# One fused two-block network on one core: SSD decays moved off GpSimd, small matmuls issued as groups, and a planner that knows the array's tilings

## Chip, cores and metric

One core of a Trainium2 chip runs the whole program as one launch. The metric is the time on the device in microseconds. The kernel before was run three times: 3711.24, 3717.8 and 3721.67 us, median 3717.8 us.

## The reference

A token stream of 512 tokens and a context of 256 tokens, 1024 channels in fp32, go through a block of two layers and then through a second block. Layer 0 is a gated-delta mixer with a mixture of experts, layer 1 an SSD mixer with a mixture of experts; both are modulated by adaLN chunks (a vector times a weight of 1024 by 6144). The second block has an S5 mixer, a short convolution and a sparse attention side by side, and a gated feed-forward. Cut to what the change touches:

```python
# gated delta: the solve that the kernel does by blocks of 32, 64 and 128
lower = where(strict, einsum('nbhid,nbhjd->nbhij', kb, kc) * decay, 0.0)
sol = triangular_solve(eye + lower, rhs, lower=True, unit_diagonal=True)
# SSD, for each of 8 groups of 4 heads, forward and backward
acs = cumsum(dt_i * A, axis=1)
seg = where(tril, acs[:, :, None] - acs[:, None, :], -inf)
wts = einsum('btgn,bsgn->btsg', c_i, b_i)[..., None] * exp(seg) * dt_i[:, None]
y = einsum('btsgr,bsgrp->btgrp', wts, x_i) + ...
# adaLN
m = silu(cvec) @ w + b
```

## The kernel before

Channels lie on the partitions, tokens on the free axis. Large products are done with each fp32 operand split into a high and a low half (`mm3`: three matmuls); the halves of a weight are made on ACT (`wh`) and on DVE, for some SSD weights on POOL (`wl`). Small products are plain fp32 matmuls, which show as two records each in the trace. A stationary operand of 32 or 64 rows or columns takes a part of the 128 x 128 array; outputs on other partitions of PSUM go to other column parts, inputs on other partitions of SBUF to other row parts.

**The planner.** The program is recorded by the class `Rec`: each call on an engine becomes an operation with its predecessors and an estimated cost. `flush` orders what was recorded and only then issues it; there are some ten flushes, one for each stage. `schedule` is a list scheduler: at each step it takes, for each engine, the first operation by rank among those that can start earliest, within a tolerance `tol`; the rank is the program's position less `beta` times the length of the chain that hangs on the operation. `flush(trials)` makes an order for each pair (beta, tol) and issues the one whose planned end is first. TensorE is planned as one engine that does one matmul after another; a matmul of few columns has a cut cost. Each engine runs its instructions in the order issued; buffers come from rings (`bufs`), PSUM has eight tiles. All DMAs are issued on SP.

**Gated-delta stage** (`gdn`, 110 to 790 us). For each of eight heads: projections, norms (`ssq`: four matmuls with ones in 32 columns), the products that make L, then the inverse of 48 blocks of 32 x 32 on POOL, and two steps that join blocks of 32 and of 64. A step has a product `pB`, a copy on ACT and a product `pU`, and for 64 also transposes `pT`; each takes six tiles of time and four (or two) diagonal blocks, which lie in different row and column parts of the array. The loop is over blocks outside and time tiles inside. A scan of six steps in two directions follows. Four of six adaLN rounds are put between heads as `side` work: a round is, for each of eight k, a weight load of 1 MB and four matmuls of 32 columns, c = 0 to 3, each recorded for itself.

**SSD stage** (`ssd`, groups from 1506 to 2100 us). For each of eight groups: for each of four heads, two rows of cumulated decays are broadcast from DRAM (R), POOL subtracts `cs` from each, DVE takes the minimum (W), ACT the exponential; POOL makes Dm = mask x dt for one direction, DVE adds the other in four steps of 128 columns and multiplies W by Dm. Then projections, states, `cb` = B'C (copied to SBUF by ACT), W times cb on DVE, and the products `py` of 64 columns, two heads side by side.

The experts' stages (842 to 1506 and up to 2755 us), the second block's mixers and its feed-forward are changed in their order alone.

Of the kernel before, what the change touches and what calls it, by code (L numbers as in the profile page):

```python
# [52 lines left out]
class Rec:  # L53
# [4 lines left out]
    def __init__(self, nc, tc):  # L58
        self.nc, self.tc = nc, tc
        self.tiles, self.ops = {}, []  # L60
        self.access = {}
        for e in ("tensor", "vector", "scalar", "gpsimd", "sync"):
            setattr(self, e, Proxy(self, e))
        self.free_at = {e: 0.0 for e in ("tensor", "vector", "scalar", "gpsimd", "sync")}
        self.dma_free = 0.0
        self.slot_times = {}
        self.seen = set()
        self.npool = 0
        self.stacks, self.left = {"left": [], "right": []}, {"left": [], "right": []}
# [55 lines left out]

    def add(self, engine, method, a, k):
        reads, writes = [], []
# [8 lines left out]
        i = len(self.ops)  # L136
# [16 lines left out]
        if engine == "tensor":  # L153
            r = ww[0]
            key = r[0] + "#pe"
            q = (key, r[1] // 32 * 32, -(-r[2] // 32) * 32, 0, 1)
            lst = self.access.setdefault(key, [])
            preds.update(j for j, _, z in lst if q[1] < z[2] and z[1] < q[2])
# [3 lines left out]
        self.ops.append(dict(e=engine, m=method, a=a, k=k, preds=preds, names=names, cost=self.cost(engine, method, reads, writes, a, k), psum=any(self.tiles.get(r[0], (0, 0, 0))[2] for r in rr + ww)))  # L162
# [54 lines left out]
    def flush(self, trials=((0.0, 30.0),)):  # L217
# [54 lines left out]
        self.span, self.seq, self.free_at, self.dma_free, times = best  # L272
        self.slot_times.update(times)
        self.seen.update(uses)
        for i in self.seq:
            o = ops[i]
            getattr(getattr(self.nc, o["e"]), o["m"])(*o["a"], **o["k"])  # L277
        self.done, self.ops, self.access = ops, [], {}

    def schedule(self, static, beta, tol):  # L280
# [13 lines left out]
        for t, lst in order.items():  # L294
            for nm in lst:
                if nm in self.seen:
                    got.add(nm)
                    slots[t].remove(max(slots[t]))
                    alloc[t].add(pos[nm])
                    nxt[t] = pos[nm] + 1  # L300
        npred = [len(o["preds"]) for o in ops]
# [17 lines left out]
        while len(seq) < n:  # L319
            best = None  # L320
            for e, c in cand.items():
                fe = free_at[e]
                eb = None
                for r in c[: self.WINDOW]:
                    i = by[r]
                    st = max(fe, ready[i])
                    if eb is not None and st >= eb[0] - tol:
                        continue
                    for nm in ops[i]["tiles"]:
                        if nm in got:  # L330
# [12 lines left out]
            if best is None:  # L343
                return math.inf, seq, free_at, dma_free, slots
# [35 lines left out]
        return max(end), seq, free_at, dma_free, slots  # L380
# [169 lines left out]
def gdn(K, H, apply, w, ba_w, conv_w, a_log, dt_b, norm_g, scr, bscr, tscr, rscr, side, xc, w_out, gate, route):  # L550
# [111 lines left out]
    for h in range(NH):  # L662
# [27 lines left out]
        for j, a in enumerate((q, k_)):  # L690
            sq = per.tile([128, TT], F32, name="sq", tag="th", bufs=2)
            s.activation(sq, a, AF.Square, scale=0.5)
            for f in range(2):
                c = 32 * (2 * j + f)
                pe.matmul(pq[c:c + 32, :], K.ones[:, 0:32], sq[:, f * 384:(f + 1) * 384], start=True, stop=True)
# [94 lines left out]
        for m in (32, 64):  # L790
# [3 lines left out]
            else:  # L794
                p = K.ps([128, 6, m], "pT")
                for d, ra, ca in cut:
                    for t in range(6):
                        if d:
                            pe.matmul(p[ra, t, :], U[ra, d, t, ra], K.ident[ra, ra], start=True, stop=True, skip_group_check=True)
                        else:  # L800
                            pe.transpose(p[ra, t, :], U[ra, d, t, ra], K.ident[ra, ra])
# [4 lines left out]
            for d, ra, ca in cut:  # L806
                for t in range(6):
                    pe.matmul(p[ra, t, :], L[ca, t, ra], Ud[ca, 1 - d, t, :] if m == 32 else U[ca, d, t, ca], start=True, stop=True, skip_group_check=True)
# [3 lines left out]
            for d, ra, ca in cut:  # L812
                for t in range(6):
                    pe.matmul(p[ra, t, :], Tr[d][ra, t, :], B[ra, t, :], start=True, stop=True, skip_group_check=True)
# [102 lines left out]
    nc.flush(GDN_TRIALS)  # L917
# [4 lines left out]
GDN_TRIALS = ((0.4, 0.0),)  # L922
# [4 lines left out]
class Mod:  # L927
# [9 lines left out]
    def round(self, r):  # L937
# [4 lines left out]
        for k in range(KT):  # L942
            wt = K.wtile(self.w[r, k], [128, 4, 512])
            for c in range(4):
                nc.tensor.matmul(p[32 * c:32 * c + 32, :], self.sc[:, k, :], wt[:, c, :], start=(k == 0), stop=(k == KT - 1))
# [161 lines left out]
def moe(K, X, ws, regions, gate, routed, keep_next, gain, fill, side):  # L1107
# [159 lines left out]
    nc.flush(((0.0, 0.0),) if two else ((0.6, 30.0),))  # L1267
# [149 lines left out]
def ssd(K, H, apply, w, wz, w_dt, conv_w, conv_b, a_log, dt_b, d_skip, norm_g, w_out, gate, keep, scr, rscr, side, route):  # L1417
# [46 lines left out]
    K.softplus(dt, a, tmp, sh, "W", 4)  # L1464
# [8 lines left out]
    for dst, ms in ((cs, (mid[:, 0, :], mid[:, 1, :])), (ea, (K.m_le, K.m_ge)), (we, (K.m_gt, K.m_lt)), (et, (K.ones, K.ones))):  # L1473
# [5 lines left out]
        s.activation(dst, p, AF.Copy if dst is cs else AF.Exp)  # L1479
    for j, x in enumerate((cs, ea)):  # L1480
# [4 lines left out]
        s.activation(rows, p.rearrange("p t i -> p (t i)"), AF.Copy)  # L1485
# [5 lines left out]
    for g in range(8):  # L1491
# [3 lines left out]
        for r in range(4):  # L1495
            h = 4 * g + r
            R = []
            for d in range(2):
                x = tmp.tile([128, 4, 128], F32, name="R", bufs=4)
                nc.sync.dma_start(x.rearrange("p t i -> p (t i)"), dbc(rscr[32 * d + h], 128))  # L1500
                g_.tensor_tensor(x, x, cs[:, :, 32 * d + h:32 * d + h + 1].to_broadcast([128, 4, 128]), op=OP.subtract)
                R.append(x)
            W = tmp.tile([128, 4, 128], F32, name="W", bufs=4)
            v.tensor_tensor(W, R[0], R[1], op=OP.min)
            s.activation(W, W, AF.Exp)
            Dm = tmp.tile([128, 4, 128], F32, name="Dm", bufs=1)
            g_.tensor_tensor(Dm, K.m_le[:, None, :].to_broadcast([128, 4, 128]), dt[:, 0:4, h:h + 1].to_broadcast([128, 4, 128]), op=OP.mult)
# [80 lines left out]
        cbs = grp.tile([128, 4, 128], F32, name="cbs", bufs=2)  # L1588
        s.activation(cbs, pcb, AF.Copy)
        for W in Ws:  # L1590
            v.tensor_tensor(W, W, cbs, op=OP.mult)
        py = [K.ps([128, 512], "py") for _ in range(2)]
        for i in range(2):
            for t in range(4):
                for r in range(2):
                    h = 2 * i + r
                    pe.matmul(py[i][64 * r:64 * r + 64, t * 128:(t + 1) * 128], xt[:, t, h * 64:(h + 1) * 64], Ws[h][:, t, :], start=(t == 0), stop=(t == 3))
# [35 lines left out]
    nc.flush(((0.3, 30.0), (0.1, 0.0), (0.6, 0.0)))  # L1633
# [29 lines left out]
    nc.flush(((0.6, 30.0), (0.8, 30.0), (0.8, 120.0)))  # L1663
# [504 lines left out]
def mix_out(K, H, I, y5, yc, ya, keep, gain):  # L2168
# [44 lines left out]
    nc.flush(((0.6, 30.0),))  # L2213
# [7 lines left out]
def ffn(K, X, H, R, I, out):  # L2221
# [28 lines left out]
    nc.flush(((0.6, 30.0),))  # L2250
# [3 lines left out]
def block2(K, X, Rs, I, scr, par, e_par, uscr, keep, out):  # L2254
# [25 lines left out]
    nc.flush(((0.0, 30.0), (0.0, 60.0), (0.3, 60.0), (0.6, 60.0)))  # L2280
# [5 lines left out]
    nc.flush(((1.0, 30.0),))  # L2286
# [198 lines left out]
```

## Time and profile before

| | |
|---|---|
| median of three runs | 3717.8 us |
| the profiled execution's own time | 3719.51 us |
| span of its instructions | 3717.7 us |
| PE busy | 3442.1 us, 93%, 21457 instructions |
| DVE busy | 1914.3 us, 51% |
| ACT busy | 1105.9 us, 30% |
| POOL busy | 662.7 us, 18% |
| mean granted TensorE clock | 0.966 |
| DMA | 669.18 MB, mean 180 GB/s |

PE is TensorE's matmuls, PEld its weight loads, DVE VectorE, ACT ScalarE, POOL GpSimd, SP SyncE. A busy time is the union of an engine's instructions. All operations are recorded through one helper, so every row has the same line, L277, and instructions are told apart by their tiles, written out<-in. "128*32 128x512" means 128 rows and 32 columns of the array and a moving operand of 512 columns. A row with "x8" stands for eight instructions of one kind one after another.

### The profile page before, as it was taken

What the parts mean: (1) busy time and instruction counts of PE and PEld (TensorE: products, weight loads), DVE (VectorE), ACT (ScalarE), POOL (GpSimd) and SP (SyncE); (2) the same over time, 40 slices, a digit from 0 to 9 for tenths busy, and PEclk for the clock granted to TensorE, in tenths of its full rate; (3) what the DMA queues carried; (4) which work ended last, traced back from release to release, by engine and by line L of the source; (5) the groups of instructions that cost most, each with busy time, mean ns of one, the idle gap of its engine ahead of it and who ended that gap; (6) DMA issues with size and microseconds to landing.
All of it is one profiled execution on the core that took longest, in us unless ns stands there. A gap on an engine that the chain in (4) does not pass through costs nothing. (4 is left out here: it accounts for less than half of the span.)

```text
span 3717.7 us, 55087 instructions
## 1 busy us (share of the span) xinstructions
PE 3442.1 (93%) x21457; PEld 2310.9 (62%) x21457; DVE 1914.3 (51%) x4006; ACT 1105.9 (30%) x2270; POOL 662.7 (18%) x849
## 2 busy tenths in 40 slices
PE   7999998899999999889999779988879999999999
PEld 4777775656444454667777664332247657878887
DVE  4657754453223222798888551371254574445552
ACT  3355443423111111433333322020032343333331
POOL 0546544301000000154444011020001000000000
PEclk9989999899999999999999889999999999999999
DMA  5422137354888887343333349899972302333332
GB/s 193 151 54 66 54 85 244 123 187 162 348 313 322 333 321 298 115 119 102 115 106 101 129 181 365 357 369 410 420 214 77 120 1 91 94 105 85 97 87 87
DMA packets 251649, 669.18 MB, mean 180 GB/s; under 512 B 72156, under 2 KB 85612, under 8 KB 202236
## 3 DMA queue, kind: packets, MB, share of 16 engines
q1 hardware_dynamic: 251388, 665.66, 50.7%
q8 instruction: 169, 2.77, 0.3%
q14 instruction: 92, 0.75, 0.1%
HBM read 644.26 MB, written 21.30 MB: 179 GB/s over the span
## 5 line engine op out<-in xcount | busy, mean ns | idle before, releaser
L277 DVE TENSOR_TENSOR wl<-w,wh 128x512 fp32r<-128x512 f32 (+3 forms) x452 | 320.9, 713 | 443.2 <-PE fu L277 67.6
L277 ACT ACTIVATE wh<-w 128x512 fp32r<-128x512 f32 (+3 forms) x500 | 307.0, 621 | 620.8 <-PE fu L277 120.6
L277 PE MATMUL eg<-we,xs 128*32 128x512 f32 (+1 forms) x1536 | 374.2, 597 | 9.5 <-DMA we<-moe_w 8.3
L277 PE MATMUL eu<-we,xs 128*32 128x512 f32 (+1 forms) x1536 | 324.4, 595 | 7.6 <-DMA we<-moe_w 7.6
L277 PE MATMUL ey<-we,hTs 128*32 128x512 f32 (+1 forms) x1536 | 295.9, 599 | 12.0 <-ACT hTs L277 9.0
L277 PE MATMUL px<-H,wl 128*128 128x512 f32 (+1 forms) x768 | 271.3, 372 | 6.4 <-DVE wl L277 6.4
L277 PE MATMUL px<-H,wh 128*128 128x512 f32 (+1 forms) x768 | 272.9, 376 | 2.8 <-ACT wh L277 1.6
L277 PE MATMUL px<-H1l,wh 128*128 128x512 f32 (+1 forms) x768 | 272.8, 369 | 0.0
L277 PE MATMUL ec<-we,xs 128*32 128x512 f32 x1024 | 237.5, 594 | 0.0
L277 DVE TENSOR_TENSOR yl<-ey,yh 64x512 fp32r<-64x512 f32 x64 | 44.1, 689 | 330.7 <-ACT yh L277 330.1
L277 POOL TENSOR_TENSOR wl<-w,wh 128x512 fp32r<-128x512 f32 x48 | 64.4, 1345 | 738.0 <-DVE H1l L277 651.5
L277 PEld LDWEIGHTS eg<-we,xs 128*32 128x32 f32 (+1 forms) x1536 | 98.7, 119 | 139.8 <-issue 94.6
L277 DVE SCALAR_TENSOR_TENSOR eth<-eth,eg 128x512 f32<-128x512 f32 x32 | 22.0, 688 | 312.9 <-ACT eth L277 312.9
L277 PEld LDWEIGHTS eu<-we,xs 128*32 128x32 f32 (+1 forms) x1536 | 94.8, 119 | 139.7 <-issue 97.2
L277 PEld LDWEIGHTS ey<-we,hTs 128*32 128x32 f32 (+1 forms) x1536 | 98.6, 120 | 120.9 <-issue 60.9
L277 PEld LDWEIGHTS px<-H,wh 128*128 128x128 f32 x768 | 146.3, 194 | 30.3 <-issue 6.4
L277 PEld LDWEIGHTS px<-H,wl 128*128 128x128 f32 x768 | 145.2, 194 | 28.9 <-DVE wl L277 8.5
L277 PEld LDWEIGHTS px<-H1l,wh 128*128 128x128 f32 x768 | 145.2, 194 | 23.3 <-issue 4.6
L277 ACT ACTIVATE eth<-eg 128x512 f32<-128x512 f32 x32 | 19.1, 596 | 463.2 <-PE eg L277 434.4
L277 PE MATMUL eyc<-we,hcTs 128*32 128x256 f32 x1024 | 143.4, 379 | 0.0
L277 POOL TENSOR_TENSOR x<-D 48x30 f32<-48x30 f32 (+14 forms) x240 | 127.1, 530 | 90.8 <-DVE D L277 73.9
L277 POOL TENSOR_TENSOR D<-D,x 48x30 f32<-48x30 f32 (+14 forms) x240 | 133.6, 557 | 17.9
(1041 smaller groups left out, 7816.1 us busy)
## 6 DMA issues: line engine op xcount, KB each, us to landing
we<-moe_w SPq DMA_DIRECT2D x384, 1024.0 KB, 7.2
w<-ada_w SPq DMA_DIRECT2D x192, 256.0 KB, 4.9
w<-w_gu SPq DMA_DIRECT2D x88, 256.0 KB, 3.0
w<-gdn_w SPq DMA_DIRECT2D x64, 256.0 KB, 3.2
w<-ssd_w SPq DMA_DIRECT2D x64, 256.0 KB, 4.0
R<-ssd_rows SPq DMA_DIRECT2D x64, 256.0 KB, 4.7
w<-w_mix SPq DMA_DIRECT2D x48, 256.0 KB, 2.7
w<-w_dn SPq DMA_DIRECT2D x40, 256.0 KB, 2.6
```

What stands on the lines that cost most here:

```text
L277: getattr(getattr(self.nc, o["e"]), o["m"])(*o["a"], **o["k"])
```

## The change

1. *SSD.* The sums `cs` are stored negated. W is made from R[0] by ACT (Identity with `cs` as bias, four instructions of 128 columns) and R[1] is joined by DVE in one step each (add cs, minimum). POOL's two kinds of decay work go. The masks are multiplied into cb (two products of 512 columns a group, from PSUM), and Dm is made after cb: ACT scales one direction by dt, DVE adds the other, and one product W by Dm replaces two. W's ring has 6 tiles in place of 4; R's has 3 and serves Dm too.
2. *Groups.* Matmuls recorded inside `nc.together()` are one operation of the plan and are issued one after another: ssq, pT, pB, pU, adaLN's four and py. For pT, pB and pU the loop is over time tiles outside and blocks inside. The transposes of pT are all matmuls by the identity.
3. *Planner.* `array` gives for each matmul its tiling, its place in the array and a time; `schedule` lets places of one tiling run side by side and adds 94 ns where the tiling changes.
4. *Trials.* Every flush takes the same 15 pairs in place of lists of one to four.

```diff
+    @contextmanager
+    def together(self):
+        assert self.run is None
+        self.run = []
+        yield
+        self.run = None
...
+        if not self.run:
+            self.run.append(len(self.ops))
+            self.record(self.run[0], engine, method, a, k)
+            self.ops[-1]["more"] = []
+        else:
+            self.record(self.run[0], engine, method, a, k)
...
+    SWITCH = 94.0
+    @staticmethod
+    def array(method, a):
...
+        size = lambda x: 32 if x <= 32 else 64 if x <= 64 else 128
+        lhs, n = a[1], free(a[2])
+        rows, cols = size(lhs.ap[0][1]), size(free(lhs))
+        r0, c0 = (x.offset // x.ap[0][0] % 128 if x.ap[0][0] else 0 for x in (lhs, a[0]))
+        wide = lhs.dtype in (F32, F32R)
+        two = lhs.dtype == F32 and method != "transpose"
+        d = (2 if two else 1) * n / 2.4 + (13.5 if lhs.dtype == F32R else 4.0)
+        if wide and cols == 128:
+            d = max(d, 109.0 * free(lhs) / 128 if lhs.dtype == F32 else 94.0)
+        elif wide:
+            d = max(d, 58.0 if cols == 64 else 30.0)
+        else:
+            d = max(d, 28.0)
+        return (rows, cols), (r0 // rows, c0 // cols), (2 if two else 1) * d
...
-    def flush(self, trials=((0.0, 30.0),)):
+    TRIALS = tuple((b, t) for b in (0.0, 0.2, 0.4, 0.6, 1.0) for t in (0.0, 30.0, 90.0))
+    def flush(self, trials=TRIALS):
...
+                    if e == "tensor":
+                        tiling, place, _ = ops[i]["pe"][0]
+                        st = max(st, held.get(place, 0.0) if tiling == mode else drained + self.SWITCH)
...
+            elif e == "tensor":
+                fin = at = st
+                for tiling, place, t in o["pe"]:
+                    if tiling != mode:
+                        if mode is not None:
+                            at = max(at, drained + self.SWITCH)
+                        mode, held = tiling, {}
+                    at = max(at, held.get(place, 0.0))
+                    held[place] = at + t
+                    drained = max(drained, at + t)
+                    fin = max(fin, at + t)
+                    at += 7.0
+                free_at[e] = max(at, held[place]) if mode == (128, 128) else at
...
-            for d, ra, ca in cut:
+            with nc.together():
                 for t in range(6):
-                    pe.matmul(p[ra, t, :], L[ca, t, ra], ...)
+                    for d, ra, ca in cut:
+                        pe.matmul(p[ra, t, :], L[ca, t, ra], ...)
...
-    nc.flush(GDN_TRIALS)
+    nc.flush()
-GDN_TRIALS = ((0.4, 0.0),)
...
-            for c in range(4):
-                nc.tensor.matmul(p[32 * c:32 * c + 32, :], self.sc[:, k, :], wt[:, c, :], ...)
+            with nc.together():
+                for c in range(4):
+                    nc.tensor.matmul(p[32 * c:32 * c + 32, :], self.sc[:, k, :], wt[:, c, :], ...)
...
-                x = tmp.tile([128, 4, 128], F32, name="R", bufs=4)
+                x = tmp.tile([128, 4, 128], F32, name="WR"[d], bufs=6 - 3 * d)
                 nc.sync.dma_start(x.rearrange("p t i -> p (t i)"), dbc(rscr[32 * d + h], 128))
-                g_.tensor_tensor(x, x, cs[:, :, 32 * d + h:32 * d + h + 1].to_broadcast([128, 4, 128]), op=OP.subtract)
                 R.append(x)
-            W = tmp.tile([128, 4, 128], F32, name="W", bufs=4)
-            v.tensor_tensor(W, R[0], R[1], op=OP.min)
+            W = R[0]
+            for t in range(4):
+                s.activation(W[:, t, :], W[:, t, :], AF.Identity, bias=cs[:, t, h:h + 1])
+                v.scalar_tensor_tensor(W[:, t, :], R[1][:, t, :], cs[:, t, 32 + h:33 + h], W[:, t, :], op0=OP.add, op1=OP.min)
             s.activation(W, W, AF.Exp)
-            Dm = tmp.tile([128, 4, 128], F32, name="Dm", bufs=1)
-            g_.tensor_tensor(Dm, K.m_le[...], dt[:, 0:4, h:h + 1].to_broadcast([128, 4, 128]), op=OP.mult)
-            for t in range(4):
-                v.scalar_tensor_tensor(Dm[:, t, :], K.m_ge, dt[:, t, 32 + h:33 + h], Dm[:, t, :], op0=OP.mult, op1=OP.add)
-            v.tensor_tensor(W, W, Dm, op=OP.mult)
             Ws.append(W)
...
-        cbs = grp.tile([128, 4, 128], F32, name="cbs", bufs=2)
-        s.activation(cbs, pcb, AF.Copy)
-        for W in Ws:
-            v.tensor_tensor(W, W, cbs, op=OP.mult)
+        cbs = [grp.tile([128, 4, 128], F32, name=f"cb{d}", bufs=1) for d in range(2)]
+        for cb_, m in zip(cbs, (K.m_le, K.m_ge)):
+            v.tensor_tensor(cb_, pcb, m[:, None, :].to_broadcast([128, 4, 128]), op=OP.mult)
+        for r, W in enumerate(Ws):
+            h = 4 * g + r
+            Dm = tmp.tile([128, 4, 128], F32, name="Dm", tag="R", bufs=3)
+            for t in range(4):
+                s.activation(Dm[:, t, :], cbs[0][:, t, :], AF.Copy, scale=dt[:, t, h:h + 1])
+                v.scalar_tensor_tensor(Dm[:, t, :], cbs[1][:, t, :], dt[:, t, 32 + h:33 + h], Dm[:, t, :], op0=OP.mult, op1=OP.add)
+            v.tensor_tensor(W, W, Dm, op=OP.mult)
...
-    nc.flush(((0.3, 30.0), (0.1, 0.0), (0.6, 0.0)))
+    nc.flush()
```

## Rows read from the trace of the kernel before

**Rows 1.** Stretches: us, busy us (count) of PE, PEld, DVE, ACT, POOL; PEclk, DMA, GB/s

```profile
110.00:790.00 680.00, 628.48 (x4571) 489.03 (x4571) 403.81 (x1105) 290.35 (x704) 321.99 (x553) 0.94 0.38 115
...
842.00:1506.00 664.00, 654.81 (x5952) 320.20 (x5952) 189.30 (x400) 117.56 (x252) 12.54 (x14) 0.99 0.77 297
...
1506.00:2100.00 594.00, 527.02 (x2845) 429.80 (x2844) 507.05 (x804) 209.50 (x370) 245.91 (x194) 0.93 0.37 115
...
2310.00:2755.00 445.00, 378.54 (x1760) 145.24 (x1757) 167.87 (x392) 66.49 (x109) 23.39 (x15) 0.97 0.95 368
```

**Rows 2.** Waits of PE, 1506 to 2100: total us, times, longest us

```profile
PE pz L277 <- POOL wl L277: 19.2, 5, 4.5
```

**Rows 3.** Instruction groups of DVE, 1510 to 2180

```profile
L277 DVE SCALAR_TENSOR_TENSOR Dm<-cst,dt,Dm 128x128 f32<-128x128 f32 x128 | 101.1, 844 | 2.6 <-POOL Dm L277 2.6
...
L277 DVE TENSOR_TENSOR W<-R 128x512 f32<-128x512 f32 x32 | 34.8, 1102 | 0.0
...
L277 DVE TENSOR_TENSOR W<-W,Dm 128x512 f32<-128x512 f32 x32 | 30.4, 949 | 0.9
...
L277 DVE TENSOR_TENSOR W<-W,cbs 128x512 f32<-128x512 f32 x32 | 24.0, 750 | 2.1 <-ACT cbs L277 2.1
```

**Rows 4.** Instruction groups of POOL, 1510 to 2180

```profile
L277 POOL TENSOR_TENSOR R<-R,cs 128x512 f32<-128x512 f32 x64 | 79.9, 1264 | 31.6 <-DMA R<-ssd_rows 15.1 <-ACT xt L277 8.5 <-DVE W L277 4.7
...
L277 POOL TENSOR_TENSOR Dm<-cst,dt 128x512 f32<-128x512 f32 x32 | 36.3, 1135 | 33.3 <-DVE W L277 27.4 <-DVE dt L277 4.4 <-DMA ssd_scratch<-y 1.5
```

**Rows 5.** Timeline, DVE and POOL: start us, us, instruction, count

```profile
1578.70 1.13 DVE L277 SCALAR_TENSOR_TENSOR Dm<-cst,dt,Dm 128x128 f32<-128x128 f32 x4
...
1701.04 2.11 POOL L277 TENSOR_TENSOR R<-R,cs 128x512 f32<-128x512 f32 x2
...
1701.11 2.70 DVE L277 SCALAR_TENSOR_TENSOR Dm<-cst,dt,Dm 128x128 f32<-128x128 f32 x4 [0.94 <-POOL Dm L277]
```

**Rows 6.** Tile vb: ns min/median/max of one, first and last start

```profile
L277 ACT ACTIVATE vb<-vT,cols x96: 386/399/407, 99.9 to 735.6; 128x128 f32<-128x128 f32 x96
```

**Rows 7.** Timeline of PE, adaLN rounds

```profile
112.65 1.06 PE L277 MATMUL ada<-w,sc 128*32 128x512 f32 x8
...
152.83 1.04 PE L277 MATMUL ada<-w,sc 128*32 128x512 f32 x2
```

**Rows 8.** Tile py: stretch 1506 to 2100 (PE, PEld, DVE), then timeline

```profile
1506.00:2100.00 594.00, 35.97 (x256) 25.02 (x256) 11.79 (x16) 0.93 0.37 115
...
1802.04 0.65 PE L277 MATMUL py<-W,xt 128*64 128x128 f32 x4
...
1803.25 0.44 PE L277 MATMUL py<-W,xt 128*64 128x128 f32 x4
```

**Rows 9.** Tile ada by stretch: PE, PEld, ACT

```profile
110.00:553.00 443.00, 16.73 (x59) 2.61 (x62) 0.60 (x1) 0.93 0.29 80
...
553.00:690.00 137.00, 49.48 (x192) 8.48 (x186) 1.79 (x3) 0.98 0.72 229
```

**Rows 10.** Tiles pB, pU and pT (in this order), 110 to 790: PE, PEld, ACT

```profile
110.00:790.00 680.00, 27.44 (x576) 22.98 (x576) 6.51 (x16) 0.94 0.38 115
...
110.00:790.00 680.00, 23.94 (x576) 21.71 (x576) 18.08 (x48) 0.94 0.38 115
...
110.00:790.00 680.00, 16.82 (x144) 13.28 (x144) 3.90 (x8) 0.94 0.38 115
```

**Rows 11.** Timeline of PE, block steps of the inverses

```profile
205.48 0.86 PE L277 MATMUL pU<-B,Td 32*32 32x32 f32 x48
...
212.67 0.92 PE L277 MATMUL pU<-B,Tr 64*64 64x64 f32 x24
...
353.14 1.21 PE L277 MATMUL pU<-B,Td 32*32 32x32 f32 x48 [0.60 <-ACT B L277]
```

**Rows 12.** Timeline of PE, cut to what began before 205.51 us

```profile
205.48 0.28 PE L277 MATMUL pU<-B,Td 32*32 32x32 f32 x4
```

**Rows 13.** Tile ssq, 110 to 790: PE, PEld, DVE, ACT, POOL

```profile
110.00:790.00 680.00, 14.06 (x56) 2.32 (x56) 0.00 (x0) 3.43 (x7) 0.00 (x0) 0.94 0.38 115
```

More of the change, by code (lines that the diff above doesn't have):

```diff
@@ L3 @@
 import math
-from contextlib import ExitStack
+from contextlib import ExitStack, contextmanager
 import numpy as np
@@ L161, in add, with free @@
         names = {r[0] for r in rr + ww}
-        self.ops.append(dict(e=engine, m=method, a=a, k=k, preds=preds, names=names, cost=self.cost(engine, method, reads, writes, a, k), psum=any(self.tiles.get(r[0], (0, 0, 0))[2] for r in rr + ww)))
+        cost = self.cost(engine, method, reads, writes, a, k)
+        pe = self.array(method, a) if engine == "tensor" else None
+        if i < len(self.ops):
+            o = self.ops[i]
+            o["preds"] |= preds
+            o["names"] |= names
+            o["cost"] += cost
+            o["more"].append((method, a, k))
+            o["pe"].append(pe)
+            return
+        self.ops.append(dict(e=engine, m=method, a=a, k=k, preds=preds, names=names, cost=cost, pe=[pe], psum=any(self.tiles.get(r[0], (0, 0, 0))[2] for r in rr + ww)))
+    SWITCH = 94.0
+    @staticmethod
+    def array(method, a):
+        def free(x):
+            n = 1
+            for s, c in x.ap[1:]:
+                n *= c
+            return n
+        size = lambda x: 32 if x <= 32 else 64 if x <= 64 else 128
[12 more added lines that the diff above has]
+        return (rows, cols), (r0 // rows, c0 // cols), (2 if two else 1) * d
     def cost(self, engine, method, reads, writes, a, k):
@@ L689, in gdn @@
         pq = K.ps([128, 384], "ssq")
[L690 to L695, printed above, removed]
+        sqs = []
+        for a in (q, k_):
+            sqs.append(per.tile([128, TT], F32, name="sq", tag="th", bufs=2))
+            s.activation(sqs[-1], a, AF.Square, scale=0.5)
+        with nc.together():
+            for c in range(4):
+                j, f = divmod(c, 2)
+                pe.matmul(pq[32 * c:32 * c + 32, :], K.ones[:, 0:32], sqs[j][:, f * 384:(f + 1) * 384], start=True, stop=True)
         sq = K.nm.tile([128, 512], F32, name="ssq_", tag="nm", bufs=3)
@@ L805, in gdn @@
             p = K.ps([128, 6, m], "pB")
-            for d, ra, ca in cut:
+            with nc.together():
                 for t in range(6):
-                    pe.matmul(p[ra, t, :], L[ca, t, ra], Ud[ca, 1 - d, t, :] if m == 32 else U[ca, d, t, ca], start=True, stop=True, skip_group_check=True)
+                    for d, ra, ca in cut:
+                        pe.matmul(p[ra, t, :], L[ca, t, ra], Ud[ca, 1 - d, t, :] if m == 32 else U[ca, d, t, ca], start=True, stop=True, skip_group_check=True)
             B = tmp.tile([128, 6, m], F32, name=f"B{m}")
@@ L811, in gdn @@
             p = K.ps([128, 6, m], "pU")
-            for d, ra, ca in cut:
+            with nc.together():
                 for t in range(6):
-                    pe.matmul(p[ra, t, :], Tr[d][ra, t, :], B[ra, t, :], start=True, stop=True, skip_group_check=True)
+                    for d, ra, ca in cut:
+                        pe.matmul(p[ra, t, :], Tr[d][ra, t, :], B[ra, t, :], start=True, stop=True, skip_group_check=True)
             for d, ra, ca in cut:
@@ L943, in round @@
             wt = K.wtile(self.w[r, k], [128, 4, 512])
-            for c in range(4):
-                nc.tensor.matmul(p[32 * c:32 * c + 32, :], self.sc[:, k, :], wt[:, c, :], start=(k == 0), stop=(k == KT - 1))
+            with nc.together():
+                for c in range(4):
+                    nc.tensor.matmul(p[32 * c:32 * c + 32, :], self.sc[:, k, :], wt[:, c, :], start=(k == 0), stop=(k == KT - 1))
         row = K.nm.tile([128, 512], F32, name="adarow", tag="nm", bufs=3)
@@ L1478, in ssd @@
             pe.matmul(p[:, :, c], ms[d], a[:, 0:n, c], start=True, stop=True)
-        s.activation(dst, p, AF.Copy if dst is cs else AF.Exp)
+        if dst is cs:
+            s.activation(dst, p, AF.Copy, scale=-1.0)
+        else:
+            s.activation(dst, p, AF.Exp)
     for j, x in enumerate((cs, ea)):
@@ L1484, in ssd @@
         rows = K.nm.tile([64, 512], F32, name="rows", tag="nm", bufs=3)
-        s.activation(rows, p.rearrange("p t i -> p (t i)"), AF.Copy)
+        s.activation(rows, p.rearrange("p t i -> p (t i)"), AF.Copy, scale=1.0 if j else -1.0)
         nc.sync.dma_start(rscr[64 * j:64 * j + 64], rows)
```

46 lines of the change are left out of this document (25 added, 21 removed).

## Prediction

> **What bounds the kernel now.** I read the busy time by stage first [rows 1]. In the gated-delta stage (110 to 790 us) PE is busy 628.48 of 680 us and no other engine passes 404. In the SSD groups (1506 to 2100 us) two engines are nearly full: PE 527.02 and DVE 507.05 of 594 us, and POOL holds 245.91. In the first expert stage (842 to 1506) PE is busy 654.81 of 664 us; in the second (2310 to 2755) the DMA share is 0.95, so transfers set it. So the change can pay in two places: less TensorE time in the gated-delta stage, less VectorE and TensorE time in SSD. The granted clock is 0.94 and 0.93 of full speed there [rows 1]: part of either stretch ran at 1.2 GHz instead of 2.4.
>
> Second, the waits: TensorE's one long wait in SSD is for the low halves of weights that POOL makes (19.2 us in 5 waits) [rows 2]; POOL works on decays and these splits in one queue.
>
> Third, single instructions. Dm on VectorE, 128 columns, has a mean of 844 ns [rows 3]. Four of them took 2.70 us while POOL worked on R and 1.13 us with POOL idle [rows 5]. The decays on POOL slow the decays on DVE.
>
> Fourth, what small matmuls cost. A group of four adaLN matmuls (eight records) took 1.06 us; a single one (two records), put alone between the projection's matmuls, took 1.04 us [rows 7]. Issued alone, each of the four costs as much as all four in one group.
>
> **SSD, part by part.** Removed from POOL: 64 subtractions (79.9 us) and 32 Dm products (36.3 us) [rows 4]. Removed from DVE: 32 minima of 512 columns (34.8 us) and 32 products W by cbs (24.0 us). Kept: 32 products W by Dm (30.4 us) and 128 Dm steps (101.1 us) [rows 3]. Added on DVE: 128 steps of 128 columns (add cs, minimum) and 16 mask products of 512 columns from PSUM. Four 128-column steps cost 1.13 us undisturbed [rows 5], so 256 cost 256 / 4 x 1.13 = 72 us; the 32 kept products cost at least 32 x 0.69 = 22 us and the 16 masks 11 us, where 0.69 us for 512 columns is my choice a little under the 750 ns mean of W by cbs [rows 3]. That is 105 us against 34.8 + 24.0 + 30.4 + 101.1 = 190 us. POOL keeps its weight splits and y sums: 245.91 - 116.2 = 130 us, half of before, so I leave half of the present excess of 85 us on them: DVE goes down by some 45 us. The bounds are 0 (POOL's rest meets them as often as now) and 85. DVE then has about 460 of 594 us and no longer stands level with PE.
>
> ACT gets 128 Identity and 128 Copy instructions of 128 columns. The nearest row, a Copy with a per-partition scale, has a median of 399 ns [rows 6]: 256 x 0.4 = 102 us, less 8 copies of cb (about 5 us). ACT is now at 209.50 of 594 us [rows 1], so some 306: the cover is idle ACT time. Without it these would stand in the chain ahead of py (second rival). The two sign changes, the deeper W ring and the softplus buffers add no instruction, and the 64 broadcast loads stay as many, now straight into the rings W and R.
>
> py: 256 records, 35.97 us busy. Four in one row of the array took 0.65 us, two pairs side by side 0.44 us [rows 8]. With a step s and a last record's tail t, 3s + t = 0.65 and s + t = 0.44, so s = 0.105 and t = 0.335 us. A group of eight pairs costs 7s + t = 1.07 us, sixteen groups 17 us: 19 us less, of which I take 18; bounds 0 and 19.
>
> The stage: py 18 us, the wait for POOL's splits 19 us (POOL's queue has lost 116 us), and 8 us for TensorE's short waits on DVE and the clock that they cost. **45 us less**, bounds 0 and 70 (all 67 us of PE idle time cannot go: the stage's start and end are serial).
>
> **Gated-delta stage.** adaLN: 192 records in 553 to 690 us cost 49.48 us and 59 in 110 to 553 cost 16.73 us [rows 9]. Grouped by eights at 1.06 us: 24 x 1.06 = 25 us and 7.4 x 1.06 = 8 us, so 24 and 9 us less. The first is in the last two heads, where other waits stand close behind, so I count half, 12 us; the second I count whole: 21 us, bounds 9 and 33.
>
> Inverses: pB 27.44, pU 23.94 and pT 16.82 us in eight heads [rows 10], 68 us; pB and pT overlap for part of that. One head of before happens to have its blocks in rotation: pU of 48 records took 0.86 us, where another head, block after block, took 1.21 us; 24 records in pairs took 0.92 us [rows 11]. At 0.86 for each of the two products of 32 rows and 0.92 for each of the three steps of 64 rows a head costs 4.5 us and eight 36 us. Of the difference of 32 us I take 25 for the overlap; bounds 0 and 32. Transposes turned into matmuls by the identity add six records a head, inside the 0.92.
>
> That four records may start together is seen at 205.47 to 205.51 us: four records of pU, all to one PSUM tile, within 0.04 us [rows 12]. The Trainium skill, TensorEngine Tiling (Array Packing), Gotcha 1: PSUM Pressure, says that different row tiles cannot access the same PSUM bank at once. By that rule the four blocks would wait for one another and the inverses would save nothing; by the row they save 25 us. The trace speaks against the rule here, and I keep a small chance for it below.
>
> The norms' ssq: 56 records in 14.06 us [rows 13], seven groups of eight at no more than the 1.06 us of a 512-column group: 7 us less.
>
> Sum: 21 + 25 + 7 = **53 us less** in this stage, bounds 9 and 72.
>
> **The order.** Each stage's list is now made with a cost for a change of tiling and chosen from 15 parameter pairs by the plan's own end time. No instruction is added. Nothing in the trace prices this. Where PE is 99% busy (first experts) or DMA at 0.95 (second experts) [rows 1], there is little to win; a worse order could lose some per cent of any stage. I take nothing and allow 40 us either way.
>
> **Sum.** The profiled execution took 3719.5 us, its span is 3717.7 and the median of the runs 3717.8. 3719.5 - 45 - 53 = **3622 us**, own range 3575 to 3665.
>
> **Rivals.**
> *The gated-delta chain sets the end, not PE.* One head goes through projection, inverse on POOL, two block steps and six scan steps in series, and two heads overlap. For it: the adaLN rounds of 553 to 690 us fill a stretch that would otherwise wait. Against: PE is busy 92% of the stage [rows 1], and POOL 322 of 680. Then 10 us remain of the 53: 3719.5 - 45 - 10 = 3664 us.
>
> *The decays stand behind cb (slower).* Dm is now made from cb, so after cb each group has 2 x 0.69 + 4 x (1.13 + 0.69) = 8.7 us of DVE work in series with its first four ACT steps, 9.5 us in all, before py may run; now only four products (2.8 us) stand there. TensorE's cover is the next group's projections, which wait for free PSUM tiles and W buffers (six, of which a group needs four). It decides once that cover is shorter than 9.5 us. If every group shows it whole, 8 x 9.5 = 76 us: 3719.5 - 53 + 76 = 3743 us, with SSD's 45 not gained. Queued behind the new ACT steps are the weights' high halves, for which the projections wait. Against: PE is busy 527.02 / 8 = 66 us in each group, of which py is 35.97 / 8 = 4.5 us [rows 1, 8], so far more than 9.5 us can stand there.
>
> *The order takes it back (no change).* The 98 us saved are 4.0% of the 2444 us outside the two stages (3717.7 - 680 - 594). If the new choices cost as much there, or in the two themselves, the time is 3719 us. For it: the pairs are chosen by a plan that knows neither POOL's hold on DVE nor the low clock.
>
> *The clock comes back too.* The two stages lose 0.06 x 680 + 0.07 x 594 = 82 us to the lower level. If denser small groups give half of it back, 3622 - 41 = 3581 us.
>
> *Row tiles of one bank wait for one another.* The 25 us of the inverses fall out: 3647 us.
>
> **How the numbers follow.** Forecast 0.54; chain 0.11; clock 0.08; bank 0.05; no change 0.10; decays behind cb, or a worse order by more than that, 0.12. A measurement here tells 0.3%, about 11 us. Faster by more: 0.54 + 0.11 + 0.08 + 0.05 = 0.78; within: 0.10; slower: 0.12. The range reaches up over the no-change case, to 3730, and leaves out the slower one (0.12); down to 3550, the forecast with SSD's bound of 70 in place of 45 and the clock's 41 (3622 - 25 - 41 = 3556), leaving some 0.05 below.
>
> **What the profile after would show.** Right: POOL near 130 us and Dm's 128-column steps near 0.3 us in SSD; adaLN and ssq in runs of eight only; pU of 48 records in under 0.9 us; the SSD groups some 45 us and the gated-delta stage some 53 us shorter. Wrong: py waiting for W, DVE still above 500 us in SSD, the scan's steps waiting for one another while PE idles, or an expert stage grown by tens of us.

## The result and the profile after

The median went from 3719.74 us (4 runs) to **3662.88 us** (4 runs, 3659.39 to 3667.67): ratio 0.984, 95% interval 0.982 to 0.9861. The profiled execution of after took 3663.3 us, its span is 3661.5. The forecast was 3622: the change is faster, by 57 us in place of 98.

Stage by stage the forecast came out very differently. The table gives stage lengths in us, worked out from the starts and ends of marker tiles in each trace: gated-delta from the first baT to the end of the route's last lgT, first experts from the first eg to the end of the last eyc, SSD from the first dtT to the end of the last py, second experts from their first eg to the end of the last ey, NSA from the first pq to the first br. Each ratio is to the kernel before timed beside that run (medians of 3719.74 to 3728.91 us). One of the four runs of kernel 3 took 4597.47 us, at a mean granted clock of 0.688, and is left out of its figures.

| kernel | gated-delta | experts 1 | SSD | experts 2 | NSA | ratio to before (95%) |
|---|---|---|---|---|---|---|
| before | 753.7 | 605.6 | 539.1 | 508.2 | 194.3 | 1 |
| after | 775.7 | 592.2 | 510.6 | 495.5 | 180.6 | 0.984 (0.982 to 0.9861) |
| 1 decays alone | 746.1 | 609.7 | 497.5 | 507.9 | 191.6 | 0.9862 (0.9839 to 0.9885) |
| 2 groups alone | 740.6 | 610.0 | 527.7 | 507.8 | 195.5 | 0.9903 (0.9882 to 0.9923) |
| 3 planner alone | 809.2 | 584.7 | 573.7 | 494.4 | 182.0 | 1.0102 (1.0085 to 1.0118) |
| 4 after, old trial in gated-delta | 804.1 | 583.6 | 513.3 | 495.5 | 180.3 | 0.9906 (0.9885 to 0.9928) |
| 5 after, nothing charged at the pick | 721.0 | 664.7 | 500.2 | 517.1 | 186.7 | 0.993 (0.9909 to 0.9951) |
| 6 decays and groups, old planner | 737.6 | 621.4 | 499.7 | 507.8 | 192.4 | 0.9858 (0.9834 to 0.9882) |
| 7 as 6, new planner in experts and NSA | 738.9 | 591.3 | 502.7 | 494.7 | 184.4 | 0.9732 (0.9712 to 0.9753) |
| 8 as 6, half the inverse loop | 692.2 | 615.2 | 503.2 | 504.3 | 191.4 | one run |
| 9 before, half the inverse loop | 722.3 | 612.0 | 541.6 | 508.3 | 191.3 | one run |
| 10 as 7, new planner without charge in gated-delta and SSD | 724.1 | 590.2 | 500.7 | 493.7 | 184.0 | 0.964 (0.9618 to 0.9663) |
| 11 after, wider tolerances in gated-delta | 716.4 | 587.9 | 514.7 | 495.9 | 180.3 | 0.9678 (0.9657 to 0.9699) |
| 12 after, switch not charged at the pick | 713.4 | 570.4 | 501.2 | 503.9 | 181.4 | 0.9637 (0.9604 to 0.9671) |

How far one profile can be trusted: before and 1 have the same gated-delta list and differ by 7.6 us there; 2, 6 and 7 share one and lie within 3.0 us.

After's gated-delta stage is 22 us *longer* than before's (forecast 53 shorter), SSD 28.5 shorter (45), and stages that were only laid out anew gave most of the rest: experts 13 and 13, NSA 14. The windows of after that answer to [rows 1]:

```profile
110.00:812.00 702.00, 586.16 (x4605) 471.51 (x4606) 409.29 (x1096) 288.43 (x701) 323.74 (x551) 0.91 0.36 110
820.00:1504.00 684.00, 657.62 (x6090) 266.21 (x6088) 218.91 (x473) 123.27 (x272) 16.39 (x18) 0.98 0.77 301
1504.00:2072.00 568.00, 501.76 (x2852) 418.24 (x2852) 441.38 (x883) 284.77 (x618) 137.03 (x98) 0.95 0.37 119
2280.00:2712.00 432.00, 369.10 (x1722) 138.19 (x1718) 168.84 (x392) 68.13 (x111) 22.77 (x15) 0.96 0.98 384
```

In the first line PE is busy 586.16 us where it was 628.48, but its idle time rose from 52 to 116 us. In the third, VectorE is down by 66 us and POOL at 137.

What was to be taken off PE was taken off. The windows of single tiles of after: pB, pU, pT and ssq, then ada in two stretches, then py; the number after the length is PE's busy time (compare [rows 8 to 10, 13]):

```profile
110.00:812.00 702.00, 16.25 (x576) 14.07 (x576) 6.54 (x16) 0.91 0.36 110
...
110.00:812.00 702.00, 16.47 (x576) 14.17 (x576) 18.07 (x48) 0.91 0.36 110
...
110.00:812.00 702.00, 10.47 (x192) 9.12 (x192) 3.93 (x8) 0.91 0.36 110
...
110.00:812.00 702.00, 5.97 (x56) 1.10 (x56) 0.00 (x0) 3.32 (x7) 0.00 (x0) 0.91 0.36 110
...
110.00:553.00 443.00, 8.98 (x64) 2.04 (x64) 0.58 (x1) 0.91 0.27 78
553.00:700.00 147.00, 37.42 (x192) 7.29 (x192) 1.73 (x3) 0.93 0.71 223
...
1504.00:2072.00 568.00, 17.03 (x256) 14.14 (x256) 11.46 (x16) 0.95 0.37 119
```

Inverses: 68.20 to 43.19 us, 25.0 less. adaLN: 7.8 and 12.1 less. ssq: 8.1 less. Together 53 us of TensorE time, as many as the forecast's sum, and the stage is not shorter. py is 18.9 less.

Instruction groups of VectorE and POOL in after's SSD, 1510 to 2150 us (compare [rows 3, 4]; POOL's groups R and Dm are gone):

```profile
L334 DVE SCALAR_TENSOR_TENSOR W<-R,cs,W 128x128 f32<-128x128 f32 x128 | 53.9, 472 | 3.8 <-DMA R<-ssd_rows 1.9 <-ACT W L334 1.8
...
L334 DVE SCALAR_TENSOR_TENSOR Dm<-cb,dt,Dm 128x128 f32<-128x128 f32 x128 | 44.9, 401 | 4.4 <-ACT Dm L334 4.0
...
L334 POOL TENSOR_TENSOR wl<-w,wh 128x512 fp32r<-128x512 f32 x48 | 67.7, 1412 | 757.6 <-PE pcx L334 656.7 <-PE dtT L334 22.2 <-DVE wl L334 21.3
```

A Dm step went from a mean of 844 to 401 ns.

### The profile page after: what moved, and what is told of

It is laid out like the page before. It is cut to its first block, busy times and chain, and to the rows that moved or that the text cites. A ratio compares the mean times of both kernels' runs of the same rounds, so it can differ in the third digit from the quotient of the medians.

```text
span 3661.5 us, 55517 instructions
## 1 busy us (share of the span) xinstructions
PE 3311.1 (90%) x21505; PEld 2205.9 (60%) x21505; DVE 1857.6 (51%) x4086; ACT 1175.8 (32%) x2518; POOL 555.1 (15%) x753
## 5 line engine op out<-in xcount | busy, mean ns | idle before, releaser
L334 PE MATMUL eg<-we,xs 128*32 128x512 f32 (+1 forms) x1536 | 289.8, 600 | 7.1 <-DMA we<-moe_w 6.0
L334 PE MATMUL eu<-we,xs 128*32 128x512 f32 (+1 forms) x1536 | 259.1, 597 | 10.7 <-DMA we<-moe_w 10.7
L334 PE MATMUL ey<-we,hTs 128*32 128x512 f32 (+1 forms) x1536 | 244.9, 603 | 14.3 <-ACT hTs L334 8.7
L334 PE MATMUL ec<-we,xs 128*32 128x512 f32 x1024 | 175.0, 592 | 0.2 <-DMA we<-moe_w 0.2
L334 PEld LDWEIGHTS eu<-we,xs 128*32 128x32 f32 (+1 forms) x1536 | 70.1, 120 | 158.3 <-issue 127.5
L334 PEld LDWEIGHTS eg<-we,xs 128*32 128x32 f32 (+1 forms) x1536 | 75.6, 119 | 147.6 <-issue 121.9
L334 PEld LDWEIGHTS ey<-we,hTs 128*32 128x32 f32 (+1 forms) x1536 | 69.2, 120 | 148.4 <-issue 112.0
L334 ACT ACTIVATE yh<-ey 64x512 fp32r<-64x512 f32 x64 | 37.9, 592 | 259.8 <-PE ey L334 245.3
```

Of the source, the lines that this page charges most:

```text
L334: getattr(getattr(self.nc, o["e"]), m)(*a, **k)
```

## The experiments

First the three parts of the change, each alone on the kernel before.

**1. Decays alone.** The hunks in the SSD function except py's, among them:
```
-                g_.tensor_tensor(x, x, cs[:, :, 32 * d + h:32 * d + h + 1].to_broadcast([128, 4, 128]), op=OP.subtract)
...
+                s.activation(W[:, t, :], W[:, t, :], AF.Identity, bias=cs[:, t, h:h + 1])
```


> The kernel before with the new SSD decays alone; its matmuls, its planner and its trials are those of before. Theory D (the decays free DVE and GpSimd, and the SSD groups are bound there): SSD's GpSimd time falls from 243 to about 135 us, the stage from the first dtT to the last py falls by 20 to 30 us of the 539, nothing else moves, whole kernel about 3695. Theory O (the 28 us that SSD won came from the new order and the grouped py): GpSimd falls as much, the stage by under 10 us, whole kernel 3710 to 3725.

Measured: 3678.22 us. SSD went from 539.1 to 497.5, more than theory D asked for; the other stages stay within 8 us. The window of SSD in this kernel, columns as in [rows 1]:

```profile
1525.00:2022.00 497.00, 480.97 (x2684) 404.10 (x2685) 404.13 (x804) 270.01 (x589) 126.21 (x90) 0.99 0.36 112
```

POOL fell to 126 us, PE is busy 481 of 497 us, its granted clock is 0.99. The decays alone won 42 us, more than the whole change won in this stage. The stage of before, for comparison:

```profile
1528.00:2067.00 539.00, 496.90 (x2670) 407.68 (x2670) 470.68 (x724) 192.96 (x342) 237.66 (x185) 0.95 0.34 103
```

PE's idle time fell from 42 to 16 us. Its busy time fell by another 16 us with the same matmuls, at a granted clock of 0.99 in place of 0.95.

**2. Groups alone.**
```
+        with nc.together():
+            for c in range(4):
```
for ssq, and likewise for ada, pB, pU, pT and py. 

> The kernel before with the small matmuls grouped alone (inverses, ssq, adaLN, py); planner, trials and decays of before. Gated-delta stage (first baT to the route's last lgT, 754 us before, 776 after). Theory A (the groups save PE time and the new order loses it again): 700 to 730 us, whole kernel about 3670 to 3695 with the py. Theory B (a chain sets the pace of the heads, PE does not): 745 to 760 us, whole kernel 3700 to 3725. Theory C (the runs of eight themselves hold PE back, since a run waits for its last input and for weights that come one after another): 770 us or more, whole kernel 3725 or more.

Measured: 3694.87 us. The gated-delta stage has 740.6 us, between the intervals of theories A and B and nearer to B: 6 to 13 us are won where 53 us of work were taken away. Theory C falls: the runs do no harm. py gave SSD 11 us. From the first baT to the last lgT PE is busy 655.1 us against 699.9 before, but idle 85.5 us against 53.8. The waits of PE that took up what was saved, before and in 2 (47 to 850 us; total us, times, longest us):

```profile
PE oT L277 <- DVE o L277: 6.8, 6, 3.0
...
PE pB L277 <- DMA Ud<-gdn_inverses: 5.0, 7, 1.7
```
```profile
PE oT L332 <- DVE o L332: 15.3, 5, 10.0
PE pB L332 <- DMA Ud<-gdn_inverses: 13.3, 5, 9.8
PE pB L332 <- DVE D L332: 12.7, 1, 12.7
```

oT waits for the scan's output, pB for the inverses and for D, the blocks that POOL's loop works on: 41 us in place of 12, all in the chain of a head.

**3. Planner alone.** `schedule`, `array` and the 15 `TRIALS` of after, with no `together` and the old decays. 

> The kernel before with the new planner alone (array model and 15 trials in every stage), no groups and the decays of before. Theory A (the new order is what lengthened the gated-delta stage): 765 to 790 us there; theories B and C: 745 to 760 us. In all three the stages that the change did not edit (both expert stages, NSA, S5) get shorter by 30 to 45 us as in the changed kernel; whole kernel 3690 to 3710 by A, about 3675 by B and C.

Measured: 3766.71 us, slower than before. Gated-delta grew by 55 us, more than theory A said, and SSD by 35, which no theory had; experts and NSA shrank by 47 us together, a little more than expected. SSD's window here:

```profile
1564.00:2138.00 574.00, 493.31 (x2673) 411.65 (x2674) 442.35 (x723) 200.42 (x340) 250.85 (x185) 0.92 0.30 95
```

The decays are those of before, so its line shown in 1 is the one to compare: PE's busy time is about the same (493 and 497 us), but it stands 81 us, against 42.

**4. The old trial.** After, in the gated-delta stage:
```
-    nc.flush()
+    nc.flush(((0.4, 0.0),))
```


> The changed kernel with one line put back: the gated-delta stage is laid out by the one trial of before (0.4, 0.0) in place of the best of 15, still with the array model. Theory A: the stage falls from 776 to 725 to 745 us, whole kernel 3610 to 3635. Theory B: about 755 us, whole kernel about 3640. Theory C: 770 us or more, whole kernel about 3660.

Measured: 3695.75 us, gated-delta 804.1. Theories A and B miss; C has the stage (770 or more) but not the total, and kernel 2 speaks against it. The 15 trials win back 28 us of what the array model costs. The longest wait of PE in this kernel's 150 to 250 us, then its windows ahead of and around it:

```profile
PE pB L334 <- DMA Ud<-gdn_inverses: 42.5, 1, 42.5
```
```profile
47.00:150.00 103.00, 101.25 (x617) 80.88 (x617) 62.35 (x150) 43.75 (x84) 9.56 (x10) 0.98 0.42 138
150.00:250.00 100.00, 50.84 (x448) 42.56 (x447) 48.11 (x112) 29.40 (x69) 69.34 (x118) 0.76 0.20 48
```

TensorE is full up to 150 us, but not with what the first head needs; then it stands for 42.5 us ahead of that head's inverses, and the stretch has a granted clock of 0.76. Something puts the head's small matmuls late. In the changed kernel it can be seen at the norms' ssq: the timeline of ACT with its last input, then that of PE:

```profile
394.78 0.85 ACT L334 ACTIVATE sq<-act_k 128x768 f32<-128x768 f32 x1
```
```profile
395.56 0.60 PE L334 MATMUL px<-H,wh 128*128 128x512 f32 x2
...
406.43 0.28 PE L334 MATMUL px<-H,wl 128*128 128x256 f32 x1
406.64 0.85 PE L334 MATMUL ssq<-sq,ones 128*32 128x384 f32 x8
```

The square is ready at 395.6 us, ssq starts at 406.6, and all that PE runs in between is projections. ssq is the first link of a head's chain (norms, GE and L, block stores, POOL's loop, inverses, scan). From the end of the last square to the start of ssq's last record it takes 0.7 to 13.0 us in after's eight heads, 20.7 and 34.7 in 4's first two. With the same groups and the old planner (6, below) it takes 0.4 to 1.0 us in seven heads and 13.7 in one. In the planner, a matmul whose tiling is not the current one may start no earlier than `drained + SWITCH`, 94 ns, and the pick prefers another that can start sooner by more than the tolerance `tol`. The 15 trials have 0, 30 and 90: none reaches 94. So (theory S) every 128x128 matmul that is ready passes a small one, however long the chain behind that is.

**5. Nothing charged at the pick.** After, without these lines:
```
-                    if e == "tensor":
-                        tiling, place, _ = ops[i]["pe"][0]
-                        st = max(st, held.get(place, 0.0) if tiling == mode else drained + self.SWITCH)
```


> The changed kernel, but the planner no longer charges the switch of tiling when it picks the next matmul; in the clock that it keeps after the pick the switch still counts. Theory S (charged at the pick, a small matmul that must switch loses to any 128x128 matmul that could start sooner, so that the head's ssq, row, pB and pU come late and the heads start late): the first head's GE moves from 102 us towards 100 or earlier, the last head's from 652 to 600 to 625, the gated-delta stage from 776 to 715 to 745, and the expert stages lose 10 to 30 us again because they switch more often; whole kernel 3600 to 3650. Theory T (not the picking, but the array model's times make the order worse): the stage stays at 765 to 800, whole kernel 3655 to 3700.

Measured: 3698.11 us. Gated-delta has 721.0, as theory S said, and the last head's GE starts at 600.4 us in place of 652.7; ssq comes at most 1.7 us after its input. The first head's GE moved the other way, from 101.7 to 105.4. But the first experts grew by 72 us, over twice what was allowed for, so that the whole kernel lies in theory T's interval though the stage does not.

**6. Both edits, old planner.** The hunks of 1 and 2 together. 

> The changed kernel's decays and groups with the planner and trials of before. If the two edits add up and the new planner only takes away in the gated-delta stage and SSD: stage gated-delta 735 to 745, SSD (first dtT to last py) 485 to 500, whole kernel about 3640 to 3650, less than the changed kernel. Rival (the new planner is what makes the two edits fit together): 3660 to 3690.

Measured: 3671.38 us, inside the rival's interval, though gated-delta and SSD lie in those of the first answer. The edits do not add up: SSD has 499.7 us where the decays alone had 497.5 (PE's wait of px for the low halves that VectorE makes rose from 3.8 to 16.1 us), and the first experts grew to 621.4. Kernels 6 and 2 have one list there; what differs is PE's wait for weights (6, then 2):

```profile
PE ey L332 <- DMA we<-moe_w: 13.0, 7, 3.0
```
```profile
PE ey L332 <- DMA we<-moe_w: 3.8, 4, 1.4
```

Why the weights came later in 6 stays open.

**7. By stage.** As 6, with the new planner where it had won (experts, NSA); elsewhere `tilings=False`:
```
+                    if e == "tensor" and self.tilings:
```


> The changed kernel's decays and groups; the expert stages and NSA laid out by the new planner, all other stages by the planner and trials of before. If what the planner does is local to a stage: gated-delta 735 to 745, SSD 485 to 500, expert stages 20 and 13 us shorter than before, NSA 12 shorter, whole kernel 3590 to 3610. Rival (what the planner wins in the expert stages came only because the gated-delta and SSD orders ended late, with the weights already loaded): expert stages as before, whole kernel about 3640.

Measured: 3624.25 us, 14 above the interval and 16 below the rival. The planner's gain in the experts is there (591.3) though gated-delta and SSD have the old orders.

**8 and 9. Half the inverse loop.** The edit, on 6 and on the kernel before:
```
-        for j in range(1, 31):
+        for j in range(1, 31, 2):
```
On 6: 

> The decays and groups with the planner of before, and GpSimd's inverse loop leaves out every second of its 30 steps (38 us a head become about 19). Theory B (after the grouping the chain store, load, GpSimd loop, inverses, scan sets the pace of the heads): the gated-delta stage falls by 30 us or more against the same kernel with the whole loop. Rival P (PE in its fixed order sets the pace, the loop is covered): under 12 us.

On before: 

> The kernel before, with GpSimd's inverse loop leaving out every second of its 30 steps, and nothing else. Theory B (the chain through that loop set the pace of the heads before the change already, so that taking small matmuls off PE could not pay in full): the gated-delta stage falls from 746 to 754 us to 720 or less. Rival P (before the change PE was the bound and the loop was covered; only the grouping uncovered it): 735 us or more.

Measured: 692.2 us against 737.6 to 740.6 (8), 45 to 48 less; 722.3 against 746.1 to 753.7 (9), 24 to 31 less, 2 us short of theory B's bound. No matmul was touched by this edit. In 8, PE's waits of pB for the inverses and D, 24 us in 6, fall to 1.3: with the groups, the chain through POOL's loop is on the path. For the kernel before this is less clear. PE waited only 5.0 us for the inverses there; in 9 its idle time is 15 us less and its busy time 16 us less, at a granted clock of 0.96 in place of 0.94. The planner, which knows the shorter loop, also put PE's matmuls in another order in both kernels, and each was run once. What the loop gave and what the order gave is not told apart, so that the chain was on the path already before the change is likely, not shown.

**10. No charge in two stages.** As 7, but in gated-delta and SSD:
```
-    nc.flush(((0.4, 0.0),), tilings=False)
+    nc.flush(charge=False)
```


> The kernel laid out by stage, with one step more: gated-delta and SSD now also by the array model and 15 trials, but without the charge for a switch at the pick; the expert stages and NSA keep the charge, the other stages the planner of before. If the stages are independent: gated-delta 715 to 730 in place of 739, the experts 590 to 600, SSD and its end 5 us shorter, whole kernel 3595 to 3610. If a gated-delta stage that ends sooner only waits for the experts' weights: the experts grow by as much as it shrinks, whole kernel about 3625.

Measured: 3590.03 us, 5 below the interval. The experts keep their 590; SSD is 2 us shorter, not 5.

**11. Wider tolerances.** After, in the gated-delta stage:
```
-    nc.flush()
+    nc.flush(tuple((b, t) for b in (0.0, 0.2, 0.4, 0.6, 1.0) for t in (150.0, 200.0, 300.0)))
```


> The changed kernel with one line changed: in the gated-delta stage the trials' tolerances are 150, 200 and 300 ns in place of 0, 30 and 90; the charge at the pick stays, 94 ns. Theory S (a tolerance below the charge lets every ready 128x128 matmul pass the small ones; one above it gives them their rank back): the stage falls from 776 to 715 to 740 us, whole kernel 3610 to 3640. If the charge at the pick harms in another way than by this rank: 760 us or more, whole kernel 3650 or more.

Measured: 3602.66 us, 7 below the interval, gated-delta 716.4; ssq comes at most 0.8 us after its input. Model and charge are unchanged; only the tolerance now passes 94. Theory S holds. The tolerance counts for the picks of all engines, though; kernel 12 changes TensorE's charge alone.

**12. Places only.** After, with one term less in the pick:
```
-                        st = max(st, held.get(place, 0.0) if tiling == mode else drained + self.SWITCH)
+                        st = max(st, held.get(place, 0.0) if tiling == mode else drained)
```


> The changed kernel, in which the pick no longer counts the 94 ns of a switch but still counts whether the place in the array is free (and, for another tiling, that the array has drained). It tells what the expert stages live from. Theory P (they gain because the pick sends neighbouring 128x32 matmuls to different column places, so that these overlap): first experts 585 to 600 us as in the changed kernel, against 665 with no charge at the pick; gated-delta 710 to 740; whole kernel 3590 to 3625. Theory W (they gain because fewer switches are made): first experts above 630 us, gated-delta 710 to 740, whole kernel 3640 to 3700.

Measured: **3589.54 us**, level with 10 and faster than both kernels of this case. Gated-delta has 713.4; the first experts 570.4, 22 below the changed kernel, though the switch is no longer charged at the pick: theory P, and more than it asked for. ssq comes at most 1.8 us after its input. The second experts are 8 us longer than in after (503.9). The instruction group ec (PE, first experts) of after, of 5 and of 12:

```profile
L334 PE MATMUL ec<-we,xs 128*32 128x512 f32 x1024 | 175.0, 592 | 0.2 <-DMA we<-moe_w 0.2
```
```profile
L334 PE MATMUL ec<-we,xs 128*32 128x512 f32 x1024 | 254.6, 594 | 0.0
```
```profile
L334 PE MATMUL ec<-we,xs 128*32 128x512 f32 x1024 | 183.2, 594 | 0.0
```

One record lasts 592 to 594 ns in all three; what differs is how many run side by side. The group is busy 70 to 80 us less than in 5. That is not time of the stage, since groups overlap; all records of 128x32 together, 5116 to 5120 in each trace, are busy 601 us in 5, 521 in after and 509 in 12. Theory W falls by the changes of tiling in the same stage, counted in the traces: 100 in after, 148 in 12, 150 in before, 246 in 5. 12 changes as often as before and is 35 us shorter. Which places of the array the matmuls took, no trace shows. PE's timeline in 12 shows two of ec and two of eg within 0.63 us:

```profile
1000.08 0.62 PE L334 MATMUL ec<-we,xs 128*32 128x512 f32 x2
1000.09 0.62 PE L334 MATMUL eg<-we,xs 128*32 128x512 f32 x2
```

What 12 mends elsewhere can be read from the first and last starts of tiles: GE (a head's block matrices), dtT (the small matmuls that the decays wait for) and py. After, then 12:

```profile
L334 DVE TENSOR_TENSOR GE<-G,E x16: 406/546/693, 101.7 to 652.7; 128x512 f32<-128x512 f32 x8, 128x256 f32<-128x256 f32 x8
...
L334 PE MATMUL dtT<-H,wh x16: 277/362/452, 1528.6 to 1633.5; 128*64 128x512 f32 x8, 128*64 128x256 f32 x8
...
L334 PE MATMUL py<-W,xt x256: 272/273/323, 1680.4 to 2038.9; 128*64 128x128 f32 x128
```
```profile
L334 DVE TENSOR_TENSOR GE<-G,E x16: 410/551/693, 103.2 to 597.9; 128x512 f32<-128x512 f32 x8, 128x256 f32<-128x256 f32 x8
...
L334 PE MATMUL dtT<-H,wh x16: 277/395/689, 1450.4 to 1470.3; 128*64 128x512 f32 x8, 128*64 128x256 f32 x8
...
L334 PE MATMUL py<-W,xt x256: 272/273/477, 1539.5 to 1951.2; 128*64 128x128 f32 x128
```

The heads' GE are spread over 551 us in after and 495 in 12. dtT takes 105 us to come through in after, 20 in 12, and the first py stands 152 and 89 us behind the stage's start.

## Why the prediction was right or wrong

**Total: right side, 41 us too low.** 3662.88 lies within the stated own range (3575 to 3665), but by errors that cancel: +75 in gated-delta, +16 in SSD, about -50 in the rest.

**SSD, -45: the mechanism was right, its terms were not.** The decays alone won 42 us where their terms (19 and 8) make 27: PE's idle time gave 26, and the clock, which the forecast had only as a part of the 8, most of the other 16 (1). POOL came down to 126 to 137 us (130 forecast), VectorE is busy 66 less in after (45), ACT 75 more (97). py lost 18.9 us of work (18), but with the new decays the stage gained nothing from it (6 against 1): a term too many. Dm's step came to 401 ns, not near 0.3 us. That only 28.5 us are left in after is the order's doing: 499.7 by the old planner, 510.6 by the new, 501.2 with the switch not charged at the pick.

**Gated-delta, -53: the failed step.** The sum of the work came out, in part by luck: adaLN's groups in 553 to 700 us cost 1.56 us each (37.42 / 24), not 1.06, so 12 us of work went where 24 were counted, and the half kept back for waits made up for it. What failed is the step from "PE is busy 628.48 of 680 us" to "PE's time is the stage's time": with the grouping alone PE's busy time fell by 45 us, but 32 of them came back as idle time, nearly all of it waits in the chain of a head, and the stage won 6 to 13 us (2). That is the rival *the gated-delta chain sets the end*, with its 10 us, to which 0.11 was given.

**The order, 0 with 40 either way: mis-sized in both directions.** In all it is worth some 7 us (ratio 0.9858 in 6, 0.984 in after), well inside the 40, but only because gains and losses cancel. It cost some 37 us in gated-delta (739 to 776) and 11 in SSD, and won 13 to 30 in the first experts, 13 in the second, 8 to 14 in NSA. That there is little to win where PE is 99% busy or DMA at 0.95 was wrong for both expert stages; in the first, PE's busy time did not tell how many matmuls ran side by side (12). The price is not the array model as such but one term of the pick (11, 12).

**The other rivals.** *Decays behind cb*: PE's waits of py for W are 3.8 us in all in 1, 3.2 in after and 10.9 at most (12), against 76; it did not happen. Its 9.5 us a group does not follow from its terms: 8.7 us and four ACT steps of 0.4 us in series are 10.3. *The clock comes back*: in SSD (0.93 to 0.95; 0.99 in 1), not in gated-delta (0.94 to 0.91, where PE waits more). *Row tiles of one bank wait*: no; with the blocks in rotation pU's 48 records take 0.62 to 0.87 us in after's eight heads. One of them in PE's timeline (compare [rows 11]):

```profile
190.54 0.86 PE L334 MATMUL pU<-B,Td 32*32 32x32 f32 x48 [3.20 <-ACT B L334]
```

By the rule of the Trainium skill, TensorEngine Tiling (Array Packing), Gotcha 1: PSUM Pressure, the inverses should have kept their 68 us; they take 43. The trace disagrees with the rule here.

## What to carry to other kernels

A list scheduler that counts a set-up cost when it *picks* lets whatever can start at once pass the small instructions that begin a long chain; count it in the clock only, but go on counting at the pick whether a place is free (5 dropped both, and the first experts grew), or give the rank a tolerance above the cost, and read in the trace how long after its last input such an instruction starts. Work taken off an engine that is 92% busy is not time taken off the stage: see which of its waits grow when the work goes, and if you shorten a suspected chain to test it, hold the order fixed. Time an edit and a new order apart; here one term of the order was worth 73 us (3662.88 to 3589.54), more than the 57 of the whole change.

## What the runs showed that was not expected

Busy time says little of a TensorE that is used in parts: in the first experts it is 99% both before and in 12, for the same matmuls in 34 us less (columns as in [rows 1]):

```profile
892.00:1498.00 606.00, 599.86 (x5436) 276.93 (x5435) 163.11 (x345) 86.00 (x173) 0.49 (x2) 1.00 0.83 322
```
```profile
848.00:1420.00 572.00, 567.68 (x5439) 199.86 (x5438) 163.44 (x348) 86.89 (x174) 0.49 (x2) 1.00 0.89 341
```

A standstill seems to be paid twice: the stretch with 4's wait of 42.5 us has a granted clock of 0.76, the one ahead of it 0.98. And VectorE's small steps did not come down to their undisturbed price when POOL's work was halved: 401 and 472 ns against 0.28 us (1.13 / 4, [rows 5]).
